# Strassen's scheme for an MLP's second product, with modulation vectors for one stream only and joined mLSTM scans

## The chip, the core and the metric

The kernel runs on one core of a Trainium2 chip. The time is that of the device, in microseconds (us), from the start to the end of one execution. TensorE (PE) does the matrix products, VectorE (DVE), ScalarE (ACT) and GpSimd (POOL) work on elements, and SyncE (SP) issues most of the DMAs. The products accumulate in PSUM, everything else lies in SBUF.

## What is computed

The reference is a block of two layers on a stream of 512 latent tokens and 256 context tokens, each with 1024 features. Layer 0 mixes by gated linear attention and grouped-query attention over all 768 tokens, layer 1 by mLSTM and retention, of which only the latent tokens' output counts. Each layer ends in an MLP with 4096 hidden units:

```python
def sq_relu_mlp(h, w1, w2):
    return jnp.square(jax.nn.relu(h @ w1)) @ w2
```

Ahead of each mixer and each MLP the rows are normalized and modulated, `rmsnorm(x, g) * (1.0 + scale) + shift`, and each branch is gated at its end. Shift, scale and gate (parts 0 to 5 of a layer) are vectors made from a conditioning vector by a product with `ada_w`, one for the latent stream and one for the context stream.

The mLSTM keeps a state per head and direction over chunks of tokens, C_t = decay x C_(t-1) + u_t, and each chunk's output is the sum of a part inside the chunk and the product of the queries with the state at its start.

## The kernel before

**Numbers in two halves.** Every large product is made in three matmuls (`mm3`, lines 463 to 468): an operand is split (`split`, 194 to 196) into a rounded copy, made by ACT (line 195), and the remainder, made by DVE (196); then hi by hi (466), hi by lo (467) and lo by hi (468) go into one PSUM bank.

**The MLP** (563 to 652) takes the 4096 hidden units in eight groups of 512. `hidden(b)` makes the group's first product: for each of four blocks f of 128 hidden units it loads and splits a block of W1 (`load1`), multiplies it with the 1024 features of all tokens in eight steps k (768 tokens are done as 512 and 256 columns in layer 0; 512 in layer 1), and `evac` takes the PSUM through relu and square into the two halves of the hidden values: relu and square on ACT (593, 597), a product and the remainder on DVE (599, 603). `second(b)` then multiplies the hidden values of each tile of 128 tokens with the group's 512 rows of W2, 512 columns at a time, 12 matmuls for each of two halves m, and adds the result to the sum `yacc` of that tile (DVE line 646; for the first group an ACT copy, 644). With the last group the tile is finished by `done`.

**Modulation vectors beside it.** While the MLP of layer 0 runs, a generator `side` makes part 5 of layer 0 and parts 0 to 5 of layer 1 (`ada_part`, 289). A step loads 256 rows of 512 columns of `ada_w` and DVE multiplies them by the conditioning values and sums (307, 309), for the latent and the context stream. At the end of 512 columns two matmuls with ones (312) sum over the partitions, and `ada_finish` adds bias and gain. Calls of `next(side)` stand behind each block of the first product and behind the tiles that `PLAN["side"]` lists, so eight steps in a group.

**The mLSTM** (`mlstm_pair`, 1328 to 1424) does two heads h at a time, in both directions d. A scan per head and direction (1367) makes the states X, head h on its own 64 partitions of a tile whose other 64 were set to zero once (1587). The output takes eight matmuls with the values inside the chunk (1403) and eight with the states (1406), these over all 128 partitions, where the zeros keep the other head out.

**Order and buffers.** Each engine works its instructions in one order, which the builder sets from the order in which the code issues them. Weights pass through `raw` tiles (three) and `wh`/`wl` tiles (five each) of the pool `w1`, and `xh`/`xl` tiles (three each) of `xw`. PSUM has two tiles of two banks (tag A), two of one (B), and the single M and O.

## Time and profile before

| what | value |
| --- | --- |
| median of three runs | 1775.58 us (1774.12 to 1779.86) |
| the profiled execution | 1774.87 us |
| its span, first to last instruction | 1773.1 us |
| mean granted clock of TensorE in it | 0.977 of full speed |
| MLP of layer 0 | about 485 to 1034 us of the span |
| mixer of layer 1 | about 1034 to 1427 us |
| MLP of layer 1 | about 1427 to 1766 us |

The span is what the profiler recorded between the first and the last instruction; the run around it is 1.8 us longer. Busy times and shares say what an engine did, not what it was needed for. Where an engine is busy without a gap the stretch is as long as its work; where several wait for each other, the chain that ended last says who was waited for. A matmul's printed duration overlaps with its neighbours, so its cost in a row of them is the distance from one start to the next.

### The profile page before, as it was taken

What the parts mean: (1) busy time and instruction counts of PE and PEld (TensorE: products, weight loads), DVE (VectorE), ACT (ScalarE), POOL (GpSimd) and SP (SyncE); (2) the same over time, 40 slices, a digit from 0 to 9 for tenths busy, and PEclk for the clock granted to TensorE, in tenths of its full rate; (3) what the DMA queues carried; (4) which work ended last, traced back from release to release, by engine and by line L of the source; (5) the groups of instructions that cost most, each with busy time, mean ns of one, the idle gap of its engine ahead of it and who ended that gap; (6) DMA issues with size and microseconds to landing.
All of it is one profiled execution on the core that took longest, in us unless ns stands there. A gap on an engine that the chain in (4) does not pass through costs nothing.

```text
span 1773.1 us, 25222 instructions
## 1 busy us (share of the span) xinstructions
PE 1702.9 (96%) x9981; PEld 1364.3 (77%) x9981; DVE 1066.6 (60%) x1687; ACT 676.0 (38%) x1201; POOL 123.0 (7%) x168
## 2 busy tenths in 40 slices
PE   7998989999999999999999999978998999999998
PEld 5785567656888888888888878767787888888886
DVE  5444566564674657658558693376787744444445
ACT  5344456553442122122121454634553542232332
POOL 0000201100000000000000000264111000000000
PEclk9999989999999999999999999989997999999999
DMA  9423443224353335235335552243544523333322
GB/s 288 124 84 105 161 144 124 72 66 155 119 167 96 107 104 171 85 106 172 101 109 166 188 182 57 83 124 118 160 125 153 196 78 106 97 99 99 99 83 107
DMA packets 170718, 220.72 MB, mean 124 GB/s; under 512 B 17484, under 2 KB 112800, under 8 KB 170600
## 3 DMA queue, kind: packets, MB, share of 16 engines
q1 hardware_dynamic: 165416, 201.28, 36.4%
q0 software_dynamic: 5184, 17.83, 2.9%
q8 instruction: 78, 1.28, 0.3%
q14 instruction: 40, 0.33, 0.1%
HBM read 193.76 MB, written 25.31 MB: 124 GB/s over the span
## 4 chain that ended last, share of the span: by engine, by line
PE 80%; DVE 7%; DMA 4%; ACT 4%; issue 3%; POOL 1%; SPq 1%; DVEq 0%; ACTq 0%; POOLq 0%
PE x L466 22%; PE x L467 21%; PE x L468 21%; PE x L976 2%; DMA x<-x 2%; PE x L953 2%; PE x L967 1%; DVE x L196 1%; DMA x<-in_mlp_w_dram 1%; PE x L312 1%; PE x L718 1%; PE x L413 1%; DMA x<-in_ada_w_dram 1%; PE x L817 1%; PE x L258 1%
## 5 line engine op out<-in xcount | busy, mean ns | idle before, releaser
L466 PE MATMUL x<-x,x 128*128 128x512 f32 (+2 forms) x2112 | 793.5, 377 | 7.5 <-ACT x L195 2.3
L467 PE MATMUL x<-x,x 128*128 128x512 f32 (+2 forms) x2120 | 790.7, 373 | 7.5 <-DVE x L196 7.5
L468 PE MATMUL x<-x,x 128*128 128x512 f32 (+2 forms) x2120 | 787.8, 373 | 0.0
L466 PEld LDWEIGHTS x<-x,x 128*128 128x128 f32 x2112 | 401.1, 190 | 100.3 <-DVE x L646 6.2
L467 PEld LDWEIGHTS x<-x,x 128*128 128x128 f32 x2120 | 402.7, 190 | 79.7 <-DVE x L196 11.8
L468 PEld LDWEIGHTS x<-x,x 128*128 128x128 f32 x2120 | 402.1, 190 | 69.2 <-issue 1.5
L195 ACT CAST x<-x 128x1024 fp32r<-128x1024 f32 (+3 forms) x247 | 230.6, 950 | 503.0 <-DMA x<-in_mlp_w_dram 233.6
L196 DVE TENSOR_TENSOR x<-x,x 128x1024 fp32r<-128x1024 f32 (+3 forms) x247 | 269.9, 1106 | 195.5 <-ACT x L195 194.1
L646 DVE TENSOR_TENSOR x<-x,x 128x512 f32<-128x512 f32 x140 | 95.8, 684 | 84.6 <-PE x L468 84.3
L309 DVE SCALAR_TENSOR_TENSOR x<-x,x,x 128x512 f32<-128x512 f32 x196 | 135.8, 746 | 5.4 <-DMA x<-in_ada_w_dram 5.3
L593 ACT ACTIVATE x<-x 128x512 f32<-128x512 f32 (+2 forms) x81 | 46.0, 589 | 139.3 <-PE x L468 131.7
L599 DVE TENSOR_TENSOR x<-x,x 128x512 f32<-128x512 f32 (+2 forms) x81 | 53.5, 677 | 73.0 <-ACT x L597 69.3
L955 DVE TENSOR_REDUCE x<-x 128x1 f32<-128x768 f32 (+1 forms) x48 | 37.0, 776 | 18.0 <-PE x L953 17.8
L976 PE MATMUL x<-x,x 128*64 128x512 f32 x112 | 44.7, 618 | 0.5 <-ACT x L970 0.2
L307 DVE TENSOR_SCALAR x<-x,x 128x512 f32<-128x512 f32 x28 | 12.9, 483 | 51.6 <-PE x L312 51.6
L956 ACT ACTIVATE x<-x,x 128x768 f32<-128x768 f32 (+1 forms) x48 | 36.3, 759 | 18.1 <-DVE x L955 18.1
L967 PEld LDWEIGHTS x<-x,x 128*128 128x128 f32 x224 | 24.6, 141 | 23.2 <-issue 21.1
L953 PE MATMUL x<-x,x 128*128 128x256 f32 (+1 forms) x160 | 37.5, 352 | 3.6 <-DMA x<-x 3.5
L603 DVE TENSOR_TENSOR x<-x,x 128x768 fp32r<-128x768 f32 (+1 forms) x48 | 39.5, 824 | 1.3
L269 POOL MEMSET x<- 128x512 f32 (+1 forms) x9 | 4.5, 505 | 510.6 <-DVE x L309 432.7
L597 ACT ACTIVATE x<-x 128x768 fp32r<-128x768 f32 (+1 forms) x48 | 35.5, 739 | 1.2
L967 PE MATMUL x<-x,x 128*128 128x128 f32 x224 | 34.1, 281 | 0.0
(305 smaller groups left out, 1503.7 us busy)
## 6 DMA issues: line engine op xcount, KB each, us to landing
x<-in_mlp_w_dram SPq DMA_DIRECT2D x128, 512.0 KB
x<-in_ada_w_dram SPq DMA_DIRECT2D x96, 512.0 KB
x<-x SPq DMA_DIRECT2D x42, 512.0 KB
x<-x SPq DMA_DIRECT2D x50, 256.0 KB
x<-in_cd_w_in_dram SPq DMA_DIRECT2D x24, 512.0 KB
x<-x POOLq DMA_DIRECT2D x36, 256.0 KB, 3.0
x<-in_ab_w_in_dram SPq DMA_DIRECT2D x16, 512.0 KB
x<-x SPq DMA_DIRECT2D x20, 384.0 KB
```

The lines of the kernel that those rows point to most:

```text
L195: self.nc.scalar.copy(hi, src)
L196: self.nc.vector.tensor_tensor(out=lo, in0=src, in1=hi.bitcast(F32), op=ALU.subtract)
L309: nc.vector.scalar_tensor_tensor(out=acc[j], in0=w, scalar=c, in1=acc[j], op0=ALU.mult, op1=ALU.add)
L466: mm(out, st[0], mv[0], start=start, stop=False)
L467: mm(out, st[0], mv[1], start=False, stop=False)
L468: mm(out, st[1], mv[0], start=False, stop=stop)
L593: nc.scalar.activation(out=h[:, c0:c1], in_=p[:, :c1 - c0], func=AF.Relu)
L599: nc.vector.tensor_tensor(out=h[:, c0:c1], in0=h[:, c0:c1], in1=p[:, :c1 - c0], op=ALU.mult)
L646: nc.vector.tensor_tensor(out=dst, in0=dst, in1=ps, op=ALU.add)
L953: mm(pS[:, s0:s1], qs[:, h * 128:(h + 1) * 128], kst[kv][i][:, s0:s1], start=i == 0, stop=i == 1)
L967: nc.tensor.transpose(pt[:, g * 128:(g + 1) * 128], P[kv][:, g, kt * 128:(kt + 1) * 128], self.C["ident"])
L976: mm(po[64 * kv:64 * kv + 64, :], av[:, kt * 128 + kv * 64:kt * 128 + kv * 64 + 64], PT[kv], start=kt == 0, stop=kt == nk - 1)
```

## The change

**The second product of groups 0 to 6** is now made by Strassen's scheme in Winograd's form. The group's values (512 hidden units by all tokens) and its rows of W2 (512 by 1024) are each cut in four blocks, by halves. Seven products of combined blocks give the four blocks of the result that eight products of single blocks gave. `weights2` loads the four blocks of W2 straight into tiles of `xw`, makes the combined ones by four subtractions on POOL, and splits seven pairs. `values2` keeps the hidden values unsplit (`hh`), makes the combined blocks on DVE and splits seven pairs into a ring of four slots. `second2` runs the seven products; each accumulates in one of two sets of banks, some on top of what an earlier product left there, and after each product its banks are added to a block of `yacc` (21 additions of 128x512 for a group of layer 0 where there were 12, 14 for one of layer 1 where there were 8; for group 0 the first writing of a block is an ACT copy). Group 7 keeps the old form.

**The order.** The blocks of the next group's first product (`hidden2`, one for each h) are issued between the products (P) of the present group, with steps of the modulation vectors (s), as strings in `PLAN["mlp"]` say, one for each layer. `PLAN["ahead"]` says how many pairs of weights and of values are made ahead of the product.

**Modulation vectors.** Parts 2 to 5 of layer 1 are made for the latent stream only, and each 512 columns of two streams or 1024 of one are finished by `ada_rows`.

**mLSTM.** One scan for a direction takes both heads on 128 partitions; the tiles are held for each parity of the pair and need no zeros. The matmuls with the states take the 64 partitions of their head, and the outputs of the two heads go to separate banks.

```diff
+    "mlp": ["PhssPsPhsPssPhsPPshs", "PhPPhPPhPhP"],
+    "ahead": (3, 3),
...
+        ns = 1 if layer == 1 and part > 1 else 2
+        md = self.T(self.dram, [2, 1024])
+        held = []
         for x in range(2):
-            acc = [self.T(pool, [128, 512], F32, tag="sp", bufs=2) for _ in range(2)]
+            acc = [self.T(pool, [128, 512], F32, tag="sp", bufs=2) for _ in range(ns)]
...
-            for j in range(2):
-                q = 32 * (2 * x + j)
-                nc.tensor.matmul(ps[q:q + 32, :], self.ones, acc[j], start=True, stop=True)
-        self.ada_finish(layer, [part], ps, 512, [[slice(32 * j, 128, 64) for j in range(2)]])
+            if len(held) == 2:
+                ps = self.pb()
+                for i, (_, _, r) in enumerate(held):
+                    nc.tensor.matmul(ps[32 * i:32 * i + 32, :], self.ones, r, start=True, stop=True)
+                self.ada_rows(layer, part, ps, [(y * 512, j) for j, y, _ in held], md)
+                held = []
...
+        def weights2(b):
...
+            sub = lambda out, x, y: nc.gpsimd.tensor_tensor(out=out, in0=x, in1=y, op=ALU.subtract)
...
+            b11, b21, b12, b22 = block(0, 0, "xh"), block(1, 0, "xh"), block(0, 1, "xh"), block(1, 1, "xl")
+            t3 = self.T(xw, [128, 1024], F32, tag="xl", bufs=3).rearrange("p (f n) -> p f n", f=2)
+            sub(t3, b22, b12)
+            sub(b12, b12, b11)
+            yield pair(b11)
+            sub(b11, b22, b12)
+            yield pair(b21)
+            sub(b21, b21, b11)
+            for x in (b11, b12, t3, b21, b22):
+                yield pair(x)
...
+        def second2(b):
...
+            for i, (c, start) in enumerate(((0, 1), (1, 1), (0, 0), (1, 1), (0, 0), (0, 0), (1, 0))):
+                while len(ws) < min(i + PLAN["ahead"][0], 7):
+                    ws.append(next(wp))
+                while len(vs) < min(i + PLAN["ahead"][1], 7):
+                    vs.append(next(vp))
...
+                for j in range(ht):
+                    for f in range(2):
+                        self.mm3(acc[j], [v[x][:, f, j * 128:(j + 1) * 128] for x in range(2)], [w[x][:, f] for x in range(2)], bool(start) and f == 0, f == 1, True)
...
+                for j in range(ht):
+                    dst = yacc2(th * ht + j)[:, ch * 512:(ch + 1) * 512]
+                    if b == 0 and new:
+                        nc.scalar.copy(dst, acc[j])
+                    else:
+                        nc.vector.tensor_tensor(out=dst, in0=dst, in1=acc[j], op=ALU.add)
+                yield
...
-        for b in range(8):
-            second(b, *hidden(b))
+        hT = []
+        for _ in hidden2(0):
+            next(side, None)
+        for b in range(7):
+            steps = {"h": hidden2(b + 1) if b < 6 else hidden(7, hT), "P": second2(b), "s": side}
+            for c in PLAN["mlp"][0 if n > 512 else 1] if b < 6 else "PsPsPsPsPsPPhshshshs":
...
+                    next(steps[c], None)
+        second(7, hT, [load2(28 + f) for f in range(4)])
...
-            for h in range(2):
-                k = slice(64 * h, 64 * h + 64)
-                X = Xs[d][h]
-                st = 1 if d == 0 else -1
-                nc.vector.tensor_tensor_scan(out=X[k][:, ::st], data0=D0[k][:, ::st], data1=U[k][:, ::st], initial=0.0, op0=ALU.mult, op1=ALU.add)
+            st = 1 if d == 0 else -1
+            nc.vector.tensor_tensor_scan(out=Xs[d][:, ::st], data0=D0[:, ::st], data1=U[:, ::st], initial=0.0, op0=ALU.mult, op1=ALU.add)
...
-                            mm(po[:, o0:o0 + 65], si[:, x], Xs[d][h][:, c::5], start=False, stop=last)
+                            mm(po[:, o0:o0 + 65], si[k, x], Xs[d][k, c::5], start=False, stop=t == 3)
```

**On PE, in the MLP of layer 0.** Before, at the end of a group's first product (tile x1078 is its last PSUM tile, written from the tokens x699 and x701 and the block of W1 x1073) follow the two matmuls with ones and then the second product into x1086:

```order
L467 MATMUL x1078_6795<-x701_3949,x1073_6785 128x256
L468 MATMUL x1078_6795<-x699_3947,x1074_6786 128x256
L312 MATMUL x1020_6355<-x1037_6518,x796_4564 32x512
L312 MATMUL x1020_6355<-x1038_6519,x796_4564 32x512
L466 MATMUL x1086_6876<-x1049_6575,x1043_6565 128x512
L467 MATMUL x1086_6876<-x1050_6576,x1043_6565 128x512
```

After, at the end of one of the seven products, which closes bank x1118 (the third tile of tokens) with the weights x1139 and x1140 and the values x1055 and x1056, a block of the next group's first product begins in x1157:

```order
L494 MATMUL x1118_7005<-x1140_7147,x1055_6515 128x512
L495 MATMUL x1118_7005<-x1139_7146,x1056_6516 128x512
L493 MATMUL x1118_7005<-x1139_7146,x1055_6515 128x512
L494 MATMUL x1118_7005<-x1140_7147,x1055_6515 128x512
L495 MATMUL x1118_7005<-x1139_7146,x1056_6516 128x512
L493 MATMUL x1157_7306<-x698_3946,x1155_7302 128x512
```

So first and second product no longer follow each other in whole groups; a block of 48 matmuls stands between two products of 18.

**On DVE, in the MLP of layer 0.** Before, additions to `yacc` (646) alternate with the modulation sums of two streams in tiles x1021 and x1022 (309), and the splits of the next group's weights (196) follow:

```order
L646 TENSOR_TENSOR x839_4873<-x839_4873,x1029_6417 128x512
L309 SCALAR_TENSOR_TENSOR x1021_6356<-x1031_6448,x7_88,x1021_6356 128x512
L309 SCALAR_TENSOR_TENSOR x1022_6357<-x1031_6448,x7_88,x1022_6357 128x512
L309 SCALAR_TENSOR_TENSOR x1021_6356<-x1034_6482,x7_88,x1021_6356 128x512
L646 TENSOR_TENSOR x843_4908<-x843_4908,x1030_6431 128x512
L309 SCALAR_TENSOR_TENSOR x1022_6357<-x1034_6482,x7_88,x1022_6357 128x512
L309 SCALAR_TENSOR_TENSOR x1021_6356<-x1034_6482,x7_88,x1021_6356 128x512
L309 SCALAR_TENSOR_TENSOR x1022_6357<-x1034_6482,x7_88,x1022_6357 128x512
L646 TENSOR_TENSOR x843_4908<-x843_4908,x1032_6451 128x512
L196 TENSOR_TENSOR x1047_6570<-x1045_6567,x1046_6569 128x1024
```

After, in group 1, the three additions behind a product (749) come together; between them stand the modulation sums (315) in x996 and x997, the split of a value block into the ring x918 (198, 768 columns) and that of a weight block (198, 1024 columns):

```order
L749 TENSOR_TENSOR x843_4880<-x843_4880,x1003_6074 128x512
L315 SCALAR_TENSOR_TENSOR x996_6057<-x999_6065,x7_88,x996_6057 128x512
L315 SCALAR_TENSOR_TENSOR x997_6058<-x999_6065,x7_88,x997_6058 128x512
L315 SCALAR_TENSOR_TENSOR x996_6057<-x999_6065,x7_88,x996_6057 128x512
L315 SCALAR_TENSOR_TENSOR x997_6058<-x999_6065,x7_88,x997_6058 128x512
L198 TENSOR_TENSOR x918_5434<-x916_5432,x917_5433 128x768
L749 TENSOR_TENSOR x841_4876<-x841_4876,x983_5952 128x512
L749 TENSOR_TENSOR x842_4878<-x842_4878,x983_5952 128x512
L749 TENSOR_TENSOR x843_4880<-x843_4880,x984_5953 128x512
L198 TENSOR_TENSOR x1009_6132<-x1007_6129,x1008_6131 128x1024
L315 SCALAR_TENSOR_TENSOR x996_6057<-x1004_6100,x7_88,x996_6057 128x512
L315 SCALAR_TENSOR_TENSOR x997_6058<-x1004_6100,x7_88,x997_6058 128x512
```

What moved is the mix: nine steps over two streams still lie in this group, beside more additions and more splits than before.

**On POOL, in the MLP of layer 0.** Before, each two memsets there belong to one finished vector (269, 270):

```order
L269 MEMSET x896_5331 128x512
L270 MEMSET x896_5331 128x512
L269 MEMSET x957_5838 128x512
L270 MEMSET x957_5838 128x512
L269 MEMSET x1018_6343 128x512
```

After, the four subtractions of a group (643) over its W2 blocks x1106 to x1110 stand between them:

```order
L329 MEMSET x1079_6712 64x512
L330 MEMSET x1079_6712 64x512
L643 TENSOR_TENSOR x1109_6976<-x1108_6974,x1107_6972 128x1024
L643 TENSOR_TENSOR x1107_6972<-x1107_6972,x1105_6968 128x1024
L643 TENSOR_TENSOR x1105_6968<-x1108_6974,x1107_6972 128x1024
L643 TENSOR_TENSOR x1106_6970<-x1106_6970,x1105_6968 128x1024
L329 MEMSET x1135_7133 64x512
```

The subtractions are new; memsets are now on 64 partitions (329, 330) and come once for each 512 columns or, later, each 1024.

## Rows read from the trace of the kernel before

**Rows 1.** The page: busy us, share, instructions of each engine; the chain.

```profile
PE 1702.9 (96%) x9981; PEld 1364.3 (77%) x9981; DVE 1066.6 (60%) x1687; ACT 676.0 (38%) x1201; POOL 123.0 (7%) x168
...
PE 80%; DVE 7%; DMA 4%; ACT 4%; issue 3%; POOL 1%; SPq 1%; DVEq 0%; ACTq 0%; POOLq 0%
```

**Rows 2.** Windows: us, busy us of PE, PEld, DVE, ACT, POOL; clock, DMA.

```profile
612.10:680.53 68.43, 68.43 (x346) 56.77 (x348) 46.28 (x64) 14.96 (x18) 1.00 (x2) 1.00 0.40 123
...
1250.00:1425.00 175.00, 165.87 (x1102) 140.32 (x1101) 137.04 (x242) 86.01 (x171) 18.02 (x31) 0.94 0.51 166
1535.00:1578.00 43.00, 43.00 (x191) 35.41 (x190) 20.04 (x26) 12.77 (x18) 0.00 (x0) 1.00 0.32 98
```

**Rows 3.** PE's timeline, first product of layer 0: start, us, instruction.

```profile
642.30 0.39 PE L467 MATMUL x<-x,x 128*128 128x512 f32 x1
...
643.43 0.28 PE L466 MATMUL x<-x,x 128*128 128x256 f32 x1
...
643.78 0.28 PE L466 MATMUL x<-x,x 128*128 128x256 f32 x1
```

**Rows 4.** The chain in layer 0's MLP: start, us, what ran.

```profile
612.10 0.98 PE x L312 x4
```

**Rows 5.** DVE's timeline in layer 0's MLP: start, us, instruction, idle before.

```profile
601.26 0.69 DVE L646 TENSOR_TENSOR x<-x,x 128x512 f32<-128x512 f32 x1
601.86 2.07 DVE L309 SCALAR_TENSOR_TENSOR x<-x,x,x 128x512 f32<-128x512 f32 x3
...
613.91 1.41 DVE L309 SCALAR_TENSOR_TENSOR x<-x,x,x 128x512 f32<-128x512 f32 x2
615.24 1.22 DVE L196 TENSOR_TENSOR x<-x,x 128x1024 fp32r<-128x1024 f32 x1
616.37 0.68 DVE L646 TENSOR_TENSOR x<-x,x 128x512 f32<-128x512 f32 x1
```

**Rows 6.** DVE groups by line and form: xcount, busy us, mean ns, idle before.

```profile
L196 DVE TENSOR_TENSOR x<-x,x 128x1024 fp32r<-128x1024 f32 x184 | 223.6, 1223 | 168.6 <-ACT x L195 167.4
...
L309 DVE SCALAR_TENSOR_TENSOR x<-x,x,x 128x512 f32<-128x512 f32 x196 | 135.8, 746 | 5.4 <-DMA x<-in_ada_w_dram 5.3
...
L646 DVE TENSOR_TENSOR x<-x,x 128x512 f32<-128x512 f32 x140 | 95.8, 684 | 84.6 <-PE x L468 84.3
...
L599 DVE TENSOR_TENSOR x<-x,x 128x768 f32<-128x768 f32 x23 | 21.9, 951 | 60.6 <-ACT x L597 60.6
```

**Rows 7.** A POOL subtraction by line and form, columns as before.

```profile
L1460 POOL TENSOR_TENSOR x<-x,x 128x512 f32<-128x512 f32 x2 | 2.6, 1282 | 1.3 <-ACT x L1459 1.3
```

**Rows 8.** All engines' timeline in the mixer of layer 1.

```profile
1226.09 2.16 DVE L1367 TENSOR_TENSOR_SCAN x<-x,x 64x325 f32<-64x325 f32 x1
...
1226.20 1.29 POOL L1460 TENSOR_TENSOR x<-x,x 128x512 f32<-128x512 f32 x1
```

**Rows 9.** The same near the end of the program.

```profile
1765.38 1.27 POOL L1668 TENSOR_TENSOR x<-x,x 128x512 f32<-128x512 f32 x1 [364.54 <-DVE x L646]
1765.55 0.69 DVE L646 TENSOR_TENSOR x<-x,x 128x512 f32<-128x512 f32 x1 [0.25 <-PE x L468]
```

**Rows 10.** DMA issues: tensors, queue, count, KB each, median us to landing.

```profile
x<-x POOLq DMA_DIRECT2D x10, 512.0 KB, 4.8
```

**Rows 11.** Line 1367: duration ns min/median/max, first and last start, form.

```profile
L1367 DVE TENSOR_TENSOR_SCAN x<-x,x x16: 826/832/2157, 1187.1 to 1281.8; 64x325 f32<-64x325 f32 x16
```

**Rows 12.** The chain in the mixer of layer 1: start, us, what ran.

```profile
1252.72 0.83 DVE x L1367
1253.56 0.83 DVE x L1367
...
1263.09 1.96 PE x L1406 x16
```

**Rows 13.** PE's timeline in the mixer of layer 0.

```profile
213.92 1.86 PE L814 MATMUL x<-x,x 64*64 64x64 f32 x48
215.71 2.51 PE L817 MATMUL x<-x,x 128*64 128x64 f32 x40
```

More of the change, by code (lines that the diff above doesn't have):

```diff
@@ L303, in ada_part @@
                     w = raw[:, k * 512:(k + 1) * 512]
-                    for j in range(2):
+                    for j in range(ns):
                         c = self.sT[:, 2 * kk + k, j:j + 1]
@@ new lines, in values2, with pair @@
+        def values2(hh, ring):
+            a11, a12, a21, a22 = (hh[:, f:f + 2, c:c + half] for c in (0, half) for f in (0, 2))
+            k = [0]
+            def pair(x, between=()):
+                c = k[0] % 4
+                k[0] += 1
+                hi, lo = [r[:, c].rearrange("p (f n) -> p f n", f=2) for r in ring]
+                if between:
+                    v = self.T(hpool, [128, n], F32, tag="h", bufs=1).rearrange("p (f n) -> p f n", f=2)
+                    op(v, *x)
+                    x = v
+                    nc.scalar.copy(hi, x)
+                    for out, i0, i1, o in between:
+                        op(out, i0 or x, i1 or x, o)
+                    op(lo, x, hi.bitcast(F32), ALU.subtract)
+                else:
+                    self.split(hi, lo, x)
+                return hi, lo
+            op = lambda out, x, y, o: nc.vector.tensor_tensor(out=out, in0=x, in1=y, op=o)
+            yield pair(a11)
+            yield pair(a12)
+            op(a21, a11, a21, ALU.subtract)
+            yield pair((a22, a21, ALU.subtract), ((a11, None, a11, ALU.add), (a12, a12, None, ALU.subtract)))
+            for x in (a11, a21, a22, a12):
+                yield pair(x)
@@ new lines, in evac2 @@
+        def evac2(f, ps, hh):
+            ps = [(p[:, max(a, c0) - c0:min(e, c1) - c0], max(a, c0), min(e, c1)) for a, e in ((0, half), (half, n))
+                  for p, c0, c1 in ps if max(a, c0) < min(e, c1)] if f == 3 else [(p[:, :c1 - c0], c0, c1) for p, c0, c1 in ps]
+            h = self.T(hpool, [128, n], F32, tag="h", bufs=1)
+            for p, c0, c1 in ps:
+                nc.scalar.activation(out=h[:, c0:c1], in_=p, func=AF.Relu)
+                nc.vector.tensor_tensor(out=hh[:, f, c0:c1], in0=h[:, c0:c1], in1=p, op=ALU.mult)
```

123 lines of the change are left out of this document (87 added, 36 removed).

## The prediction

> **What bounds the kernel now.** I read the page's busy shares and its chain first [rows 1]: TensorE (PE) is busy 96% of the span and carries 80% of the chain that ended last. VectorE (DVE) stands at 60%, ScalarE (ACT) at 38%, GpSimd (POOL) at 7%. Then the windows by stage [rows 2]: in the MLP of both layers PE is busy for the whole stretch at clock 1.00, while DVE works 46 of 68 us in layer 0 and 20 of 43 in layer 1. So there every PE instruction taken away shortens the end, as long as nobody else becomes late. In the mixer of layer 1 (1250 to 1425) PE is busy 95%. The other engines have room on average; whether they have it at the right moment is what decides the size.
>
> **PE work removed.** The seven products take fewer matmuls of 512 columns. Per group a product over half the tokens, half the columns and half the hidden units is 3 tiles x 2 x 3 = 18 matmuls, so 7 x 18 = 126 in place of 144 in layer 0, and 7 x 12 = 84 in place of 96 in layer 1. Seven of the eight groups do it: 7 x 18 + 7 x 12 = 210 fewer. The built program agrees, with 70 fewer on each of the three lines of mm3. The PE timeline gives the price by spacing, not by the printed duration, because matmuls overlap: five from 642.30 to 643.43, 0.226 us each [rows 3]; in layer 1, where 191 recorded ones fill 43.00 us, 0.225 [rows 2]. So 126 x 0.226 = 28.5 us in layer 0 and 84 x 0.226 = 19.0 in layer 1. The 256-column ones stand 0.117 apart [rows 3].
> The modulation vectors need 20 matmuls with ones where there were 28. The chain gives 0.98 us for a pair [rows 4], so 8 x 0.49 = 3.9 us. Together 28.5 + 19.0 + 3.9 = 51.4 us, all on the path.
>
> **What DVE gets in layer 0.** Its spacing in a busy stretch is shorter than its durations: an add of 512 columns to the next instruction 0.60 us (601.26 to 601.86), a weight split of 1024 columns 1.13 (615.24 to 616.37), two steps of the modulation sum 1.33, so 0.665 each (613.91 to 615.24) [rows 5]. For 768 columns I take 0.87, between the first two. A group then has 21 adds (12.6), 11 weight splits, four of W1 and seven of W2 combinations (12.4), 11 passes over half a value block (9.6) and four Relu products at their mean of 0.95 [rows 6] (3.8): 38.4 us. The modulation sums come on top. A step over both streams is four passes, 2.66 us; over the latent stream alone two, 1.33; finishing a vector is two passes of 512 columns, 1.2. The first 24 steps in the after-program are two-stream, and nine of them fall into group 0, nine into group 1, four into group 2.
> On PE a group took 68.4 us with two pairs of 0.98 [rows 2, 4]; less 18 x 0.226 = 4.1 that is 64.3, or 63.4 with one pair. DVE against that: group 0, whose first 12 adds are ACT copies, 31.2 + 23.9 + 1.2 = 56; group 1, 38.4 + 23.9 + 2.4 = 65; group 2, 38.4 + 10.6 + 6.7 + 2.4 = 58; later groups about 51. Only group 1 is at the limit by this count.
>
> **What POOL adds.** Each group gets four subtractions of 128x1024 on POOL, which had nothing but two memsets there. No row shows that size: 512 columns took 1.28 us [rows 7], so I estimate 2 x 1.28 = 2.6 us, 10.2 per group. POOL itself has room. Its cost is on DVE. At 1226.09 a DVE scan, 0.83 us as a rule, took 2.16, with a POOL subtraction of 1.29 us starting 0.11 us into it [rows 8]; an add with one operand in PSUM beside such a POOL instruction kept its 0.69 [rows 9]. So instructions with both operands in SBUF wait for POOL, and the adds and Relu products (16.4 us of a group) do not.
> The Trainium skill, "SBUF — State Buffer", section "SBUF: two separate sides", states this as an exclusive lock: the port pair is held for the whole instruction, and an instruction of DVE with two SBUF inputs is fully blocked by one on POOL that reads SBUF. The rows agree (2.16 against 0.83, 0.69 unchanged), and by the rule taken literally the whole 10.2 us would go to DVE's account.
> Bounds: 0 (all four meet adds or an idle DVE) to 10.2. I take 7, since about 70% of DVE's time in these groups is in two-operand SBUF work. Then group 0 needs 63, group 1 72, group 2 65, later ones 58, against PE's 63 to 64. Weights and values are made three products ahead, so a group may run late by some us before PE sees it. I book 9 us of waits for groups 0 to 2 and 3 for the other four: **12 us**, between 4 (pieces late at the turns only) and 25 (group 1 late by its whole excess with 11, and the others 14).
>
> **SP's queue.** The loads keep their number and size (four W2 blocks of 512 KB in place of four). In the after-program W2 blocks of the next group stand among this group's modulation loads, most of a group ahead, in slots that splits set free. A 512 KB load landed in 4.8 us [rows 10], against some 60 us of PE work between: nothing, or 4.8 per group if that cover were gone.
>
> **Layer 1's MLP.** The window shows PE without a gap [rows 2], so a group of 192 matmuls takes 192 x 0.226 = 43.4 us, and 180 will take 40.7. DVE: 11 x 1.13 + 15 x 0.60 + 14 x 0.60 = 29.8, with POOL 37. It fits. What is left is the turn of each group, where the first product of the next group needs a value slot that the last one frees, and between them lies one split: 0 to 1.22 us [rows 6] each for seven groups. I take 0.35 each, **2.5 us** (0 to 8.5), since the program puts first-product matmuls between.
>
> **The joined scans and halved matmuls.** Eight scans over 128 partitions take the place of 16 over 64, whose median is 0.832 us [rows 11]. If their time goes by columns, which are unchanged, DVE saves 8 x 0.83 = 6.6 us; if it went by partitions, nothing. The chain has two of them back to back, 0.83 and 0.83 [rows 12], so for some pairs both are on the path; I count half, 3 us. The state product used 128 rows of which half were zeros: eight matmuls (16 records) take 1.96 us on the chain [rows 12], 16 us for all. With 64 rows the nearest are two products of 64 columns, 48 records in 1.86 us with 64 rows and 40 in 2.51 with 128 [rows 13]: 0.039 against 0.063, though the former also has half the output rows. So between no gain and 38% of 16 = 6 us; I take 2.
> The Trainium skill, "TensorE: Matmul & The Clock Gate", section "Part 3: Packing small matmuls — row/col tiling", says that matmuls on different row groups of the array run at the same time. No row here has such pairs of different halves; by it the 16 us would halve, a gain of 8 where I take 2, and the sum would be 6 lower.
> Together **-5 us**, between +3 (the new order of that section costs something) and -12. The four memsets that go are on POOL, off the path. Start and end of the kernel keep their code, as the eighth group does.
>
> **Sum.** Against the profiled execution's 1774.9 us (span 1773.1): 1774.9 - 51.4 + 12 + 2.5 - 5 = 1733. Its time is 0.7 below the median of the runs, so 1734 on that scale.
>
> **Rivals.**
> *(a) Nobody is late.* DVE's spacing holds, POOL meets PSUM work, the buffers cover group 1. Then 1774.9 - 51.4 - 5 = 1718.5, with 4 us of turns 1722, and 1714.5 if the halved matmuls give 6 in place of 2. For it: DVE's 38 to 51 us in five groups of seven; against it: group 1.
> *(b) DVE is late in most groups.* Spacing as read, but the whole 10.2 us on DVE: group 0 is late by 3, group 1 by 11, group 2 by 4, each later one by some 2 for pieces in the wrong order, layer 1 by 1.5 per turn: 3 + 11 + 4 + 8 + 10 = 36, and of the scans' gain 3 is left: 1774.9 - 51.4 + 36 - 3 = 1756.5. PE's clock may add to it: it was 0.94 on average where PE idled 5% and 1.00 where it did not [rows 2]; 0.5% on some 800 us is 4.
> *(c) Slower: DVE becomes the bound in every group.* DVE needs its full durations (0.684, 1.223, 0.746, 0.951 [rows 6]) and each POOL instruction blocks it for all of its time. Then the 38.4 of a group become 42.4 and a two-stream step 2.98. Group 1: 42.4 + 26.9 + 2.4 + 10.2 = 82 against 64, so +18; group 0 +9, group 2 +10, groups 3 to 5 +3 each; layer 1: 33.4 + 10.2 = 43.6 against 40.7, +2.9 in seven groups, 20. Sum 66, and no gain from the scans: 1774.9 - 51.4 + 66 = 1789.5. It decides from 62 us of waits, 4.4 per group of the 14, since then the 51.4 + 5 and the 0.3% that a measurement of this kernel can tell from no change are used up. Against it: the spacing is shorter than the durations [rows 5, 6]. With 51 to 62 us of waits the time is the same.
> *(d) The change doesn't do what it says:* the matmul count in the built program speaks against it, 1775.
>
> **Chances.** Forecast (1725 to 1745) 0.53; (a) 0.18; (b) 0.19, with its upper part up to 1768; same 0.04 (waits of 51 to 62 us); (c) 0.05; (d) 0.01. So faster by over 0.3% 0.90, within 0.04 + 0.01 = 0.05, slower 0.05. The range goes from 1716, in the lower part of (a), to 1762, past the middle of (b) with its clock; outside lie about 0.05 below and 0.15 above. The other 0.80 is what the range should hold.
>
> **What would show it.** In the profile after: PE's spacing unchanged, 210 fewer matmuls; in layer 0's groups 1 and 2 idle time of PE before products, ended by DVE splits (L198) or POOL, up to some 5 us per group, and nearly none in groups 3 to 6; a light group of 63 us; a layer 1 group of about 41; DVE two-operand instructions of 2 us and more beside POOL's L643, adds at 0.69; scans of 0.83 on 128 partitions; L1549 shorter than 1.96 per eight. I am wrong if PE idles in layer 1's groups by more than 1.2 us each, if POOL's subtraction takes far from 2.6 us, or if the waits in groups 3 to 6 are as long as in group 1.

## The result and the profile after

| | before | after |
| --- | --- | --- |
| median of the runs | 1777.55 us (1774.12 to 1779.86) | 1750.57 us (1745.55 to 1760.33) |
| the profiled execution, its span | 1774.87, 1773.1 | 1750.84, 1749.1 |

The ratio is 0.9856, with a 95% interval of 0.9809 to 0.9903: faster by 1.4%, some 24 to 27 us. The forecast was 41 (1734 us, range 1716 to 1762). The sign and the range held; 14 to 17 us of the gain are missing.

The page after gives, as [rows 1] did, the busy time of each engine, and the chain by engine:

```profile
PE 1655.9 (95%) x9755; PEld 1322.8 (76%) x9755; DVE 1254.2 (72%) x1877; ACT 744.3 (43%) x1296; POOL 271.9 (16%) x226
...
PE 44%; DVE 6%; DMA 2%; issue 2%; ACT 1%; POOL 1%; SPq 0%; DVEq 0%; ACTq 0%; POOLq 0%
```

PE lost 47 us of work, DVE went from 60 to 72%, POOL from 7 to 16%. To see where the 24 us of span went, both spans are cut at the same four events: the first relu of layer 0's MLP, the start of its last addition to the sum, the first relu of layer 1's MLP, and the start of its last addition. First the windows of the kernel before (columns as in [rows 2]: length, busy PE, PEld, DVE, ACT, POOL, then PE's clock):

```profile
489.10:1034.20 545.10, 542.24 (x2738) 450.00 (x2736) 367.26 (x533) 144.72 (x209) 6.99 (x14) 1.00 0.43 132
1034.20:1430.80 396.60, 371.53 (x2271) 307.15 (x2272) 265.06 (x428) 190.91 (x359) 84.09 (x109) 0.94 0.41 131
1430.80:1765.50 334.70, 334.70 (x1502) 276.17 (x1501) 157.46 (x218) 103.86 (x163) 0.12 (x1) 1.00 0.31 95
```

and the same stretches after:

```profile
489.00:1024.00 535.00, 515.95 (x2595) 426.62 (x2593) 478.16 (x625) 180.90 (x269) 83.95 (x48) 1.00 0.42 131
1024.00:1422.20 398.20, 369.16 (x2271) 305.32 (x2272) 256.26 (x417) 188.97 (x356) 90.81 (x108) 0.93 0.43 131
1422.20:1741.60 319.40, 317.55 (x1418) 260.77 (x1417) 242.09 (x326) 137.78 (x201) 65.40 (x26) 1.00 0.31 98
```

| stretch | before | after | measured | forecast |
| --- | --- | --- | --- | --- |
| MLP of layer 0 | 545.1 | 535.0 | -10.1 | -28.5 - 3.9 + 12 = -20.4 |
| tail of layer 0 and mixer of layer 1 | 396.6 | 398.2 | +1.6 | -5 |
| MLP of layer 1 | 334.7 | 319.4 | -15.3 | -19.0 + 2.5 = -16.5 |

Layer 1's MLP came out as worked out. Against the forecast, layer 0's lost 10 us and the mixer 6.6. In layer 0's MLP PE was idle for 2.9 us before (545.10 less 542.24) and is now for 19.1. Four windows inside the MLPs say where: the first is groups 0 to 2, the second the rest of layer 0, the third one undisturbed group of layer 0 and the fourth one of layer 1:

```profile
512.00:755.00 243.00, 227.06 (x1120) 184.30 (x1119) 225.59 (x284) 79.50 (x112) 42.38 (x25) 0.99 0.40 122
755.00:1024.00 269.00, 267.31 (x1344) 223.19 (x1343) 231.73 (x316) 95.06 (x147) 33.26 (x18) 1.00 0.43 139
845.00:908.00 63.00, 63.00 (x324) 53.27 (x323) 58.52 (x73) 20.53 (x27) 12.32 (x9) 1.00 0.41 131
1535.00:1575.70 40.70, 40.70 (x180) 33.47 (x180) 31.62 (x42) 16.98 (x24) 10.38 (x5) 1.00 0.33 103
```

Of 243 us PE is idle 15.9 in the first window and 1.7 of 269 in the second; a later group of layer 0 runs without a gap, and a group of layer 1 takes 40.70 us for 180 matmuls, the same 0.226 each as before [rows 3]. So the missing time lies in the three groups that still sum two streams. Who was waited for there, in the list of PE's waits in layer 0's MLP (total us, times, longest):

```profile
PE x L319 <- DVE x L315: 6.4, 2, 3.5
PE x L493 <- ACT x L197: 3.2, 4, 1.7
PE x L319 <- DVE x L695: 2.8, 2, 1.7
PE x L495 <- DVE x L198: 2.5, 3, 1.2
```

The matmuls with ones (L319) stand in front with 9.2 us: 6.4 ended with a modulation sum (L315), 2.8 with a Relu product (L695) that stands among these sums in DVE's order. Then come the halves of the weights (L197, L198). One such wait, around 700 us, in the timeline of all engines:

```profile
698.10 3.55 DVE L315 SCALAR_TENSOR_TENSOR x<-x,x,x 128x512 f32<-128x512 f32 x2
...
698.42 5.42 POOL L643 TENSOR_TENSOR x<-x,x 128x1024 f32<-128x1024 f32 x2 [7.47 <-DMA x<-in_mlp_w_dram]
...
701.57 0.41 DVE L695 TENSOR_TENSOR x<-x,x 128x256 f32<-128x256 f32 x1
701.90 3.15 DVE L315 SCALAR_TENSOR_TENSOR x<-x,x,x 128x512 f32<-128x512 f32 x2
...
704.45 1.28 PE L319 MATMUL x<-x,x 128*32 128x512 f32 x3 [3.52 <-DVE x L315]
```

Two subtractions on POOL run from 698.42 to 703.8. The sum on DVE that began at 698.10 and its successors, about 0.67 us apart in a free stretch [rows 5], take 3.55 us for two and again 3.15 for two. Only the product with a PSUM operand (L695) between them is short, with 0.41. The ones matmul needs the last of these sums, and PE stood 3.52 us with the next product behind it in its queue.

### The profile page after: what moved, and what is told of

The parts are those of the page before. It is cut to its first block, busy times and chain, and to the rows that moved or that the text cites. A ratio compares the mean times of both kernels' runs of the same rounds, so it can differ in the third digit from the quotient of the medians.

```text
span 1749.1 us, 25218 instructions
## 1 busy us (share of the span) xinstructions
PE 1655.9 (95%) x9755; PEld 1322.8 (76%) x9755; DVE 1254.2 (72%) x1877; ACT 744.3 (43%) x1296; POOL 271.9 (16%) x226
## 4 chain that ended last, share of the span: by engine, by line
PE 44%; DVE 6%; DMA 2%; issue 2%; ACT 1%; POOL 1%; SPq 0%; DVEq 0%; ACTq 0%; POOLq 0%
PE x L493 13%; PE x L495 13%; PE x L494 13%; DMA x<-x 1%; DVE x L198 1%; PE x L1546 1%; DVE x L749 1%; PE x L1685 1%; PE x L1684 0%; PE x L440 0%; ACT x L197 0%; PE x L1549 0%; PE x L1517 0%; PE x L1384 0%; DVE x L433 0%
## 5 line engine op out<-in xcount | busy, mean ns | idle before, releaser
L493 PE MATMUL x<-x,x 128*128 128x512 f32 (+2 forms) x2042 | 767.0, 377 | 13.3 <-ACT x L197 6.6
L494 PE MATMUL x<-x,x 128*128 128x512 f32 (+2 forms) x2050 | 765.7, 374 | 6.7 <-DVE x L198 6.6
L495 PE MATMUL x<-x,x 128*128 128x512 f32 (+2 forms) x2050 | 762.3, 374 | 3.2 <-DVE x L198 2.9
L198 DVE TENSOR_TENSOR x<-x,x 128x1024 fp32r<-128x1024 f32 (+4 forms) x373 | 404.6, 1104 | 172.9 <-ACT x L197 171.6
L197 ACT CAST x<-x 128x1024 fp32r<-128x1024 f32 (+4 forms) x373 | 330.4, 910 | 447.1 <-PE x L494 172.1
L643 POOL TENSOR_TENSOR x<-x,x 128x1024 f32<-128x1024 f32 x56 | 147.5, 2635 | 477.4 <-DMA x<-in_mlp_w_dram 240.5
L749 DVE TENSOR_TENSOR x<-x,x 128x512 f32<-128x512 f32 x225 | 144.0, 678 | 3.1 <-PE x L495 2.5
L315 DVE SCALAR_TENSOR_TENSOR x<-x,x,x 128x512 f32<-128x512 f32 x140 | 127.1, 937 | 5.1 <-DMA x<-in_ada_w_dram 4.4
L694 ACT ACTIVATE x<-x 128x512 f32<-128x512 f32 (+4 forms) x96 | 46.0, 479 | 112.7 <-PE x L495 75.2
L695 DVE TENSOR_TENSOR x<-x,x 128x512 f32<-128x512 f32 (+4 forms) x96 | 51.4, 535 | 13.8 <-ACT x L694 13.6
L1112 PEld LDWEIGHTS x<-x,x 128*128 128x128 f32 x224 | 24.6, 141 | 23.2 <-issue 21.1
L1326 POOL DMA_DIRECT2D x<-x x16 | 9.0, 564 | 192.7 <-ACT x L1321 173.2
L680 DVE TENSOR_TENSOR x<-x,x 128x768 f32<-128x768 f32 (+3 forms) x42 | 32.6, 818 | 0.1
```

The lines of the kernel that those rows point to most:

```text
L197: self.nc.scalar.copy(hi, src)
L198: self.nc.vector.tensor_tensor(out=lo, in0=src, in1=hi.bitcast(F32), op=ALU.subtract)
L315: nc.vector.scalar_tensor_tensor(out=acc[j], in0=w, scalar=c, in1=acc[j], op0=ALU.mult, op1=ALU.add)
L493: mm(out, st[0], mv[0], start=start, stop=False, skip_group_check=partial)
L494: mm(out, st[0], mv[1], start=False, stop=False, skip_group_check=partial)
L495: mm(out, st[1], mv[0], start=False, stop=stop, skip_group_check=partial)
```

## The experiments

The theory after these readings: the missing 10 us of layer 0 are DVE's time blocked by POOL's subtractions. The rival: DVE has too much work of its own in groups 0 to 2. A third question is where the mixer's gain went. All numbers of the stretches in this table are cut as above.

| kernel | ratio to before (95%) | median | MLP 0 | mixer | MLP 1 |
| --- | --- | --- | --- | --- | --- |
| changed, again (e0) | 0.9883 (0.9852 to 0.9914) | 1751.3 | 536.3 | 397.9 | 319.4 |
| no subtractions (e1) | 0.9747 (0.9708 to 0.9786) | 1726.8 | 514.7 | 394.1 | 318.8 |
| subtractions unread (e2) | 0.9974 (0.9956 to 0.9992) | 1767.2 | 550.7 | 402.7 | 319.1 |
| one stream (e3) | 0.9781 (0.9756 to 0.9806) | 1734.2 | 519.9 | 397.4 | 319.4 |
| ones late (e4) | 0.9981 (0.9964 to 0.9998) | 1769.8 | 553.4 | 400.3 | 319.4 |
| mLSTM alone, on before (e5) | 0.9997 (0.9981 to 1.0013) | 1773.1 | 544.5 | 396.8 | 334.8 |
| vectors by turns (e6) | 0.9873 (0.9845 to 0.9902) | 1751.1 | 532.2 | 399.0 | 319.3 |
| subtractions on DVE, layer 0 (e8) | 0.9821 (0.9791 to 0.9852) | 1743.2 | 523.3 | 401.0 | 319.4 |
| subtractions on DVE (e9) | 0.9791 (0.9757 to 0.9825) | 1740.1 | 524.4 | 399.7 | 318.8 |
| the same, POOL's queue (e10) | 0.9798 (0.9765 to 0.9831) | 1740.6 | 522.4 | 399.1 | 318.8 |
| the same, by turns (e11) | 0.9767 (0.9731 to 0.9804) | 1735.9 | 517.3 | 403.1 | 318.9 |
| subtractions on DVE, by turns (e12) | 0.9771 (0.9755 to 0.9788) | 1733.9 | 517.4 | 399.1 | 318.9 |

### The changed kernel again

> The changed kernel again, beside the next three. Both theories: about 1750 us (its runs so far went from 1745 to 1760), the MLP of layer 0 535 us from the first relu to the last addition, of which about 22 us are waits that the kernel before did not have; the scans' section 11 us shorter, and the mixer of layer 1 as a whole no shorter.

It came out as expected: 1751.34 us, layer 0's MLP 536.3. The kernels that follow are set against it. The next three ran on the same chip, the others on other chips; there the ratio to the kernel before, taken on the same chip each time, is the safer figure.

### Without the subtractions

```diff
-            sub(t3, b22, b12)
-            sub(b12, b12, b11)
             yield pair(b11)
-            sub(b11, b22, b12)
             yield pair(b21)
-            sub(b21, b21, b11)
-            for x in (b11, b12, t3, b21, b22):
+            for x in (b11, b12, b12, b21, b22):
```

> The four subtractions of W2 blocks on POOL are left out, so three of the seven weight pairs are plain blocks; all else stays. Theory lock (POOL's subtractions block DVE, about 48 us of DVE time in layer 0's MLP, and PE waits for that): the added wait of 22 us falls below 8, the start of layer 1's MLP gets back some 4 us, total about 1732 us. Theory load (DVE has simply too many sums of two streams in groups 0 to 2): PE still waits some 10 us there, total about 1743.

1726.77 us, 24.6 less than the changed kernel, and layer 0's MLP 21.6 less. That stretch is then 514.7 against 512.7 for the forecast's work alone (545.1 - 28.5 - 3.9), so next to nothing of the added waits is left. Groups 0 to 2, the same window as above, have PE idle for 1.3 us in place of 15.9:

```profile
512.00:755.00 243.00, 241.67 (x1215) 198.58 (x1214) 214.37 (x301) 81.39 (x114) 5.93 (x12) 1.00 0.44 134
```

The lines by form give the size of the blocking. With the subtractions (columns as in [rows 6]):

```profile
L198 DVE TENSOR_TENSOR x<-x,x 128x1024 fp32r<-128x1024 f32 x226 | 287.4, 1277 | 141.3 <-ACT x L197 140.7
...
L643 POOL TENSOR_TENSOR x<-x,x 128x1024 f32<-128x1024 f32 x56 | 147.5, 2635 | 477.4 <-DMA x<-in_mlp_w_dram 240.5 <-DVE x L198 128.7 <-DVE x L315 36.0
...
L315 DVE SCALAR_TENSOR_TENSOR x<-x,x,x 128x512 f32<-128x512 f32 x140 | 127.1, 937 | 5.1 <-DMA x<-in_ada_w_dram 4.4
```

and without:

```profile
L198 DVE TENSOR_TENSOR x<-x,x 128x1024 fp32r<-128x1024 f32 x226 | 275.0, 1223 | 151.6 <-ACT x L197 151.2
...
L315 DVE SCALAR_TENSOR_TENSOR x<-x,x,x 128x512 f32<-128x512 f32 x140 | 100.1, 745 | 7.3 <-DMA x<-in_ada_w_dram 6.7
```

Each sum of L315 took 0.19 us more with them, and 140 of them 27 us; a weight split 0.05 more. By the page, DVE was busy 1254.2 us with them; without them it was 1197.9:

```profile
PE 1651.1 (96%) x9755; PEld 1320.5 (77%) x9755; DVE 1197.9 (69%) x1877; ACT 744.6 (43%) x1296; POOL 123.7 (7%) x170
```

So 147.5 us of POOL's work came with 56.3 us of blocking. About 48 of it lies in layer 0's MLP (the excess of each instruction over the lower quartile of its form), 6.9 a group, and about 8.6 in layer 1's.

### The subtractions on POOL, their results unread

```diff
             sub(t3, b22, b12)
-            sub(b12, b12, b11)
+            sub(t3, b12, b11)
             yield pair(b11)
-            sub(b11, b22, b12)
+            sub(t3, b22, b12)
             yield pair(b21)
-            sub(b21, b21, b11)
-            for x in (b11, b12, t3, b21, b22):
+            sub(t3, b21, b11)
+            for x in (b11, b12, b12, b21, b22):
```

> The same four subtractions run on POOL at the same places, but into a tile that nobody reads; the weight pairs are plain blocks. Theory lock: the time stays near the changed kernel's, 1746 to 1752 us, since DVE is blocked as before. If PE waits because the combined blocks come late from POOL, it falls to that of the kernel without subtractions.

This misses both: 1767.16 us, 16 above the changed kernel. Late results can't be the reason here, since nobody waits for one. But the subtractions are not at the same places either: in the changed kernel the third and fourth wait for splits that still read their blocks; unread they follow one another. POOL's timeline in group 1 has all four in one row, DVE's has five sums in the same stretch, and PE's the ones matmul that waits for the last:

```profile
625.69 10.99 POOL L643 TENSOR_TENSOR x<-x,x 128x1024 f32<-128x1024 f32 x4 [3.92 <-DMA x<-in_mlp_w_dram]
```

```profile
629.78 8.77 DVE L315 SCALAR_TENSOR_TENSOR x<-x,x,x 128x512 f32<-128x512 f32 x5
```

```profile
637.95 2.58 PE L319 MATMUL x<-x,x 128*32 128x512 f32 x4 [7.08 <-DVE x L315]
```

Five sums that take 3.3 us in a free stretch took 8.77, and PE stood for 7.08. So the blocking alone, without any data behind it, makes PE wait. DVE was hardly blocked longer in all than in the changed kernel: over layer 0's MLP it was busy 483.9 us, there 479.3. What grew is PE's idle time, 28.4 us in place of 19.5, and its busy time, 522.3 in place of 516.8, with more of the stretch at the lower granted clock (last section). That the closeness of the four subtractions is the reason is read from this place; no run varied it alone. Nor does this kernel show that late results cost nothing in the changed one: there ACT waited four times, 18.2 us together, for a subtraction before it could cast a block in layer 0. PE's waits for casts and for the remainders made after them (L197, L198) are 5.7 us in all.

### One stream

```diff
-        ns = 1 if layer == 1 and part > 1 else 2
+        ns = 1
```

> All seven modulation vectors are summed for the latent stream only (the context stream gets the same values), so 24 steps lose two passes each: 32 us less on DVE in groups 0 to 2 of layer 0's MLP, and 8 matmuls with ones fewer (3.9 us of PE). POOL's subtractions stay. Theory load: the waits in groups 0 to 2 (18 us) all but vanish, total 1728 to 1733 us with the 3.9. Theory lock: most of them stay, total about 1742.

1734.15 us, 17.2 below the changed kernel, of which 3.9 are ones matmuls. Layer 0's MLP keeps 519.9 - (512.7 - 3.9) = 11 us of added waits of 22 to 24. So either taking the blocking or taking the heavy steps away relieves PE, and taking the blocking does more. How much of this is DVE's own load stays open, since this kernel also loses sums that were blocked: by the same measure as above about 37 of the 48 us of blocking are left in layer 0's MLP.

### The ones matmuls one step later

```diff
                 yield
+                if kk == 0:
+                    if self.late:
+                        self.late.pop()()
+                    acc = [self.T(pool, [128, 512], F32, tag="sp", bufs=2) for _ in range(ns)]
+                    held += [(j, x, acc[j]) for j in range(ns)]
...
+                def finish(held=held):
+                    ps = self.pb()
...
+                self.late.append(finish)
```

> The matmuls with ones and the finishing of a vector are issued one step later in the changed kernel; nothing else moves. Theory head of the queue (PE stands at the ones matmuls, 9.3 us, with other work behind them that is ready): total 6 to 9 us less, about 1743. Rival (DVE's lateness reaches PE at the next product anyway): the wait moves to the products' splits, total 1748 to 1752.

Neither: 1769.83 us, 18.5 slower than the changed kernel. The waits at the ones matmuls (L323 here) fell from 9.2 to 3.8 us, as hoped, but those for ACT's casts (L197) rose from 3.2 to 20.5:

```profile
PE x L498 <- ACT x L197: 20.5, 8, 9.3
PE x L323 <- DVE x L318: 2.5, 2, 1.9
...
PE x L323 <- DVE x L700: 1.3, 1, 1.3
```

The finishing of the vector moved with the matmuls, and with it its stores in SP's queue. In group 0, SP's timeline, then ACT's, then PE's:

```profile
579.54 0.52 SPq L345 DMA_DIRECT2D x<-x  x2
581.26 0.39 SPq L604 DMA_DIRECT2D x<-in_mlp_w_dram  x1
```

```profile
585.68 2.94 ACT L197 CAST x<-x 128x1024 fp32r<-128x1024 f32 x3 [11.71 <-DMA x<-in_mlp_w_dram]
```

```profile
586.78 0.80 PE L498 MATMUL x<-x,x 128*128 128x512 f32 x1 [9.29 <-ACT x L197]
```

The store (L345) waits for DVE's last finishing step at 579.5. Behind it in SP's queue stands the load of W1 for the next block (L604), which goes out at 581.26; ACT has waited 11.71 us for it when it casts it at 585.68, and PE has waited 9.29 us for the cast. A wait in a DMA queue took the place of the wait removed. What the later matmuls would give with the stores out of SP's queue was not tried.

### The mLSTM part alone

This is the kernel before with `mlstm_pair` of the changed kernel and its tiles; of the diff above the prediction it has the last two pieces, and with them the new places of the outputs and no zeroing.

> The kernel before with the mLSTM part of the change alone: joined scans, states on half the partitions, no zeroing. Theory given back: the section from the first in-chunk product to the last state product shortens by about 10 us (104 to 94), and the rest of the mixer lengthens by 6 to 9 because it then waits for its own loads, total 1770 to 1774 against 1773 to 1777 of before. Rival (the give-back in the changed kernel comes from the MLP's new instructions): the gain stays, total 10 us below before.

As the first theory said: 0.9997 of before. From the first in-chunk product to the last state product it takes 95.7 us in place of 104.1, and from there to the first relu of the next MLP 135.8 in place of 127.8. That second stretch as a window, in the kernel before and then in this one:

```profile
1303.00:1430.80 127.80, 122.52 (x809) 105.16 (x808) 96.24 (x173) 58.88 (x106) 11.28 (x21) 0.92 0.51 166
```

```profile
1294.30:1430.10 135.80, 125.97 (x816) 108.84 (x813) 96.81 (x173) 59.31 (x106) 11.26 (x21) 0.90 0.49 158
```

PE is idle 9.8 us of it in place of 5.3, and busy 126.0 in place of 122.5 at a lower mean clock. So of the 8 us given back 4.5 are waits and 3.5 are longer busy time. The chain there shows what it meets: a load on which the transposes (L1474) wait, and a load of output weights:

```profile
1305.63 7.97 DMA x<-x
1313.64 1.11 PE x L1474 x4
...
1323.58 3.60 DMA x<-in_w_out_dram
```

So 8 us of the mixer's give-back are its own, since no line of the MLP changed in this kernel. That these loads are what holds it is read from the chain; no run moved one. In the changed kernel that stretch takes 140.7 us (in its second run 140.1), and without the subtractions 136.5, so about 4 us more come with the subtractions. The first of them in layer 1's MLP run while the norms ahead of it are still at work. DVE's timeline and POOL's there, with a norm step of 1.28 us that takes 3.47 and a product with the gain (L433) of 1.23 that takes 2.13:

```profile
1379.57 3.47 DVE L450 SCALAR_TENSOR_TENSOR x<-x,x,x 128x1024 f32<-128x1024 f32 x1
...
1384.26 2.13 DVE L433 TENSOR_TENSOR x<-x,x 128x1024 f32<-128x1024 f32 x1
```

```profile
1379.56 5.74 POOL L643 TENSOR_TENSOR x<-x,x 128x1024 f32<-128x1024 f32 x2 [15.18 <-DMA x<-in_mlp_w_dram]
```

These two steps were blocked for 3.1 us. That moving the subtractions off POOL gives the 4 us back is not shown: in the four profiles with the subtractions on DVE, further down, the stretch takes 141.7, 137.9, 139.9 and 137.0 us. Which of the loads would have to come earlier to keep the 8 us was not tried.

### The vectors by turns

```diff
-                    for layer, part in ((0, 5),) + tuple((1, p) for p in range(6)):
+                    for layer, part in ((0, 5), (1, 2), (1, 0), (1, 3), (1, 1), (1, 4), (1, 5)):
```

> The vectors are summed in another order, one of two streams and one of one stream by turns (part 5 of layer 0, then 2, 0, 3, 1, 4, 5 of layer 1), so the 24 heavy steps spread over five groups in place of three; the same instructions in all. Theory: waits come from groups in which DVE's work plus POOL's blocking is above PE's, so levelled it falls from 23 us to about 10 in layer 0, total about 1738. Rival: waits come wherever a subtraction meets a needed split, whatever the level: 1747 to 1752.

The rival: 1751.14 us, the same as the changed kernel. Layer 0's MLP is 3 to 4 us shorter in the profiled execution, which the runs don't confirm. With POOL's blocking in place, levelling buys nothing that can be told from zero.

### The subtractions on DVE

```diff
-            sub = lambda out, x, y: nc.gpsimd.tensor_tensor(out=out, in0=x, in1=y, op=ALU.subtract)
+            sub = lambda out, x, y: (nc.vector if n > 512 else nc.gpsimd).tensor_tensor(out=out, in0=x, in1=y, op=ALU.subtract)
```

> In layer 0 the four subtractions of a group run on DVE itself (4 x 1.13 us) and not on POOL, where they blocked DVE for about 6.9 us a group. Theory lock: DVE's account falls by some 16 us, PE's added wait in layer 0 from 23 to about 14, total about 1742. Rival (they cost DVE more in its queue than beside it, since POOL's blocking partly met idle time): 1750 or more.

1743.16 us, 8 below the changed kernel and as the theory said; layer 0's MLP waits 10.6 us in place of 23.6. Then in both layers (`nc.vector` alone in that line):

> All subtractions of W2 blocks on DVE, in both layers. Theory lock: layer 0's MLP as with layer 0 alone (523 us), layer 1's MLP still 319, since its groups leave DVE idle, and the stretch ahead of it 1 to 3 us shorter than the changed kernel's because nothing on POOL blocks the norms of that stretch: total about 1741. Rival: in layer 1, where POOL's blocking met idle time, the subtractions on DVE cost more than there: MLP of layer 1 322 or more, total 1746.

1740.11 us, and layer 1's MLP is not longer. The two kernels differ by less than their runs do. The gain expected ahead of layer 1's MLP did not come: from the last state product to the first relu it is 141.7 us, against 139.9 with the subtractions on DVE in layer 0 only. The lines by form and the page of this kernel:

```profile
L315 DVE SCALAR_TENSOR_TENSOR x<-x,x,x 128x512 f32<-128x512 f32 x140 | 100.1, 745 | 1.0 <-DMA x<-in_ada_w_dram 0.7
L643 DVE TENSOR_TENSOR x<-x,x 128x1024 f32<-128x1024 f32 x56 | 68.4, 1222 | 5.9 <-DMA x<-in_mlp_w_dram 2.8 <-DVE x L198 2.7
```

```profile
PE 1654.4 (95%) x9755; PEld 1323.4 (76%) x9755; DVE 1259.5 (72%) x1933; ACT 744.0 (43%) x1296; POOL 123.7 (7%) x170
```

The subtraction takes 1.222 us on DVE against 2.635 on POOL, and the sums are back at 0.745. DVE's busy time is 1259.5, no less than the changed kernel's 1254.2: the 61.6 us that it now spends on subtractions replace 56.3 of standing blocked. What changed is the place. By the same measure of blocking next to nothing is left of it in the MLPs. In layer 0, where PE waits for DVE, the blocking was 48 us and the subtractions are 28 x 1.22 = 34; in layer 1 they are more than the blocking was, but there DVE has time.

### The finishing DMAs through POOL's queue

```diff
-            nc.sync.dma_start(out=bt[r], in_=self.a["ada_b"][layer:layer + 1, part * 1024 + c:part * 1024 + c + 512])
+            nc.gpsimd.dma_start(out=bt[r], in_=self.a["ada_b"][layer:layer + 1, part * 1024 + c:part * 1024 + c + 512])
...
-            nc.sync.dma_start(out=md[j:j + 1, c:c + 512], in_=bt[32 * i:32 * i + 1])
+            nc.gpsimd.dma_start(out=md[j:j + 1, c:c + 512], in_=bt[32 * i:32 * i + 1])
```

> As e9, and the small loads and stores that finish a modulation vector go through POOL's DMA queue and not through SP's, where a store that waited for DVE stood ahead of W1's loads (46.7 us of SP's waiting). Theory SP's head of the queue: the weights come earlier and part of the 10 us that layer 0's MLP still waits goes, MLP of layer 0 517 to 520 us, total about 1737. Rival: those loads had time to spare in the changed kernel's order, no change from e9 beyond 1 us.

The rival: 1740.63 against 1740.11. SP's waits at those stores are gone, and PE's waits are the same. So at this place of the finish the weights had time to spare; SP's queue cost something only where the finish came later. This kernel then took 10.7 us from the last addition to the end in place of 7.9, for which no run gives a cause.

### By turns, with the subtractions on DVE

> As e10, and the vectors are summed in the levelled order (two streams and one stream by turns). With the blocking gone DVE's own work in groups 0 to 2 is all that is left; levelled it fits into PE's time (63 against 64 us a group): MLP of layer 0 514 to 517 us, total about 1734. Rival: the order makes no difference, as with POOL's subtractions.

1735.88 us, 4.8 below the one before, with layer 0's MLP at 517.3 in place of 522.4. The same without POOL's queue, which is e9 and the line of the vectors by turns together:

> Subtractions on DVE in both layers (as e9) with the levelled order of vectors (as e6), and the finishing DMAs back on SP's queue. Theory: levelling gives 5 us once nothing blocks DVE (517 us for layer 0's MLP, as in e11), and the end takes 7.9 us as in e9 and not 10.7, so about 1734 us, 0.976 of before. Rival (it was POOL's queue that gave e11 its gain): as e9, 1740.

1733.85 us (1732.45 to 1734.68), 0.9771 of before, with an interval of 0.9755 to 0.9788 that lies wholly below that of the changed kernel. Layer 0's MLP, as a window from its first relu to the start of its last addition:

```profile
488.50:1005.90 517.40, 511.60 (x2594) 425.51 (x2592) 461.67 (x653) 180.89 (x269) 9.88 (x20) 1.00 0.43 136
```

PE is idle 5.8 us of it, where it was 19.1 in the changed kernel. Without POOL's subtractions, levelling shortens this stretch by 5 us (e10 to e11) and 7 us (e9 to e12). By the ratios the gain is 0.31 and 0.20% of the time before, about 5.5 and 3.5 us. In both pairs the intervals overlap, so that no pair by itself shows a gain in time; the two agree in sign and with the stretch. This is the fastest kernel of the study that does all the work, 17 us below the changed one.

## Why the prediction was right, and which terms were off

The sign, the removed work of PE and the cause of the new waits (DVE blocked by POOL) were right. The time lies in the range, but above the forecast's own band of 1725 to 1745: two terms of the sum, the waits of layer 0 and the mixer, were too kind by 10 and 7 us, and it was the width of the range that held them.

- **PE's work.** Right. Spacing stayed 0.226, the groups of layer 1 take 40.70 us (worked out: 40.7) and an undisturbed one of layer 0 63 (worked out: 63.4).
- **DVE's work.** Right: 58.5 us busy in a later group of layer 0, blocking included, where 51 + 7 = 58 was worked out. POOL's subtraction takes 2.635 us (estimate 2.6). The blocking is 6.9 us a group in layer 0, where I took 7, and 1.2 in layer 1, where I took 7 as well; why so little there, no run shows. This is the exclusive lock that the prediction cited from the Trainium skill ("SBUF — State Buffer", "SBUF: two separate sides"); the kernel without subtractions and that with unread ones agree with it, but the cost is not the whole of POOL's time: 56.3 of 147.5 us.
- **What PE waits for that.** This step failed in size. It said "Weights and values are made three products ahead, so a group may run late by some us before PE sees it", and booked 9 us for groups 0 to 2 and 3 for the rest. The rest had 1.7. Groups 0 to 2 had PE idle for 15.9, and layer 0's MLP was 22.3 us longer than its work: 16 of this is added idle time, the other 6 is busy time of PE, which no run divides further. The lead covers most of the weights and values, but the matmuls with ones have none: they stand in PE's queue right behind the sums that they need, and 9.2 us of the waits are at them. I had counted them only as PE's work. The range for this term, 4 to 25, held it.
- **The mixer.** The scans behaved as said (median 0.835 us over 128 partitions, one of 2.16), and the state products gave more than taken. By the timeline eight of them, 16 records, now begin 1.14 us before the next instruction, where it was 1.96 [rows 12]:

```profile
L1509 DVE TENSOR_TENSOR_SCAN x<-x,x x8: 827/835/2162, 1176.5 to 1262.2; 128x325 f32<-128x325 f32 x8
```

```profile
1247.33 1.21 PE L1549 MATMUL x<-x,x 64*128 64x65 f32 x16
1248.47 1.78 PE L1546 MATMUL x<-x,x 128*128 128x65 f32 x14
```

That is a factor of 0.58, and 6.6 us for all, where I took 2. The Trainium skill ("TensorE: Matmul & The Clock Gate", "Part 3: Packing small matmuls — row/col tiling") says that matmuls on different row groups run at the same time; the trace agrees, with 0.58 against the half that the prediction worked out by it. No run separates the turns between the two halves from the smaller number of rows, with which, and half the output rows too, [rows 13] had 0.039 us against 0.063. The section came out 11 us shorter in this profile, not 5; in all the profiles with this part it is 6 to 11 shorter. What failed is the step from there to the end: I put this gain on the path without asking what is late next. The mLSTM part alone gives 8 us back, with loads on its chain, and some 4 us more come with the subtractions, whose effect I had looked for only inside the MLPs.
- **Layer 1's MLP.** -15.3 against -16.5, right.
- **The rivals.** The result lies between the forecast and rival (b) at 1756.5. In groups 0 to 2 it is near (b), with 15.9 us of idle time against 18; the waits that (b) has in the later groups and in layer 1 did not come. None of the three signs of being wrong came up: PE idles 1.9 us in all of layer 1's MLP, a subtraction takes 2.635 us, and the later groups wait far less than the first.

## What to carry to other kernels

Moving a two-input elementwise step from DVE to POOL did not free DVE here: it stood blocked 56 us, where the steps cost 62 on DVE itself, and at moments that nobody chose. When work is taken from the engine that bounds, look for every instruction in its queue that waits for another engine without a lead, however small, and for the loads that the next stage will now meet earlier. Try an edit again once another has relieved the same engine: levelling moved the median by 0.2 us beside POOL's subtractions and by 4.8 without them (e10 to e11). In layer 0's MLP the two gains are nearer to each other, 3 to 4 us and 5 to 7, so that one edit made room for the other is a hint and not shown.

## What the runs showed of the hardware that was not expected

A wait of PE cost more than its length here. In the kernel with unread subtractions the granted clock, last column but two, falls to 0.50 for the 5.7 us behind the wait of 7.08 us, and is back after it:

```profile
620.00:630.70 10.70, 10.70 (x59) 9.09 (x57) 10.51 (x13) 0.98 (x2) 5.92 (x4) 1.00 0.25 87
637.90:643.60 5.70, 5.66 (x11) 2.85 (x12) 4.77 (x7) 1.35 (x2) 0.00 (x0) 0.50 0.60 181
643.60:650.00 6.40, 6.40 (x30) 5.32 (x29) 5.27 (x9) 0.52 (x1) 0.00 (x0) 0.99 0.49 150
```

0.50 is the lower of the two levels, 1.2 GHz; the stretch did 11 recorded matmuls, ones among them, where the one ahead did 59 in 10.7 us. Over all of layer 0's MLP this kernel has 8.9 us more idle time of PE than the changed kernel (e0) and is 14.4 us longer; with the ones matmuls late it is 11.1 us more idle time and 17.1 us longer. The mean granted clock there is 0.98 in both, against 0.99.

And DVE and POOL took turns. In the same kernel the four subtractions in a row (from 625.69) end at 628.38, 631.19, 633.93 and 636.68, and four sums end 0.55 us after each of them, with the next subtraction begun 0.07 to 0.08 us after the one before. So POOL did not shut DVE out for the whole row.

The runs of the changed kernel spread over 15 us, and again over 10, where those of before spread over 6 to 13 in the several sets; with the subtractions on DVE and the vectors by turns (e12) the five runs lie within 2.3. No run shows the cause of that.
